# Column-form products in runs: all high parts of the weights first, then all low parts, in a two-layer decoder trunk

## The chip, the cores and the metric

The kernel runs on one core of a Trainium2 chip. The metric is the device time of one execution in microseconds (us). The engines are TensorE (PE, with its weight loads PEld), VectorE (DVE), ScalarE (ACT), GpSimd (POOL) and SyncE (SP), each with an instruction queue of its own that runs in order.

## The reference

256 tokens, model width 1024, one memory of 256 rows, all in float32. Cut to what matters:

```python
# layer 0
h = rms_norm(x, norm_mix[0])
b_gate, c_gate, u = jnp.split(h @ conv_w_in[0], 3, axis=-1)
z = c_gate * u                                  # then a causal conv of width 3 along the tokens
x = x + (b_gate * conv(z)) @ conv_w_out[0]
x = x + mem_cross_attention(rms_norm(x, norm_mem[0]), rms_norm(mem, norm_memkv[0]), ...)   # 4 heads of 256
g, u = jnp.split(rms_norm(x, norm_ffn[0]) @ ffn_w_gu[0], 2, axis=-1)                        # 2 x 2816 columns
x = x + (jax.nn.silu(g) * u) @ ffn_w_down[0]
# one shared K/V from x (8 heads of 128, partial rotary)
# layer 1: block attention over that K/V, then memory attention and SwiGLU as above
return rms_norm(x, norm_final)
```

With 256 tokens there is one block, so the block attention is plain causal attention.

## The kernel before

**Products.** Each float32 weight piece is loaded as `raw` (512 KB, SP's queue) and split in two: `hi`, a rounded copy that ACT writes (a cast), and `lo`, the rest, that DVE writes (raw minus hi). Activations are split in the same way and stand transposed, 128 features on the partitions, in units of four blocks of 128 features (`mix_0`, `mix_1`; in each block the high half and the low half of 256 tokens lie side by side). A product x*w is then x_hi*w_hi + x_lo*w_hi + x_hi*w_lo.

Two forms of product exist. In the row form (`mm3`) tokens come out on the partitions: three products of 256 or 512 columns for each k. In the column form (`mm_cols`, L425) the weights' 128 output columns come out on the partitions. For each of the eight k one product of `hi` with both halves of x (512 columns) and one of `lo` with x's high half (256 columns) are accumulated into one buffer, whose two halves are summed behind it (`col_sum`: an ACT copy of one half, a DVE sum with the other). Column form are the conv's input projection (`cu` for c and u, `pb` for b), the query projection of the memory attention (`q_acc`), and SwiGLU's gate and up (`gu`).

**Buffers.** The `cu` and `gu` accumulations take one of the buffers of the tag `gu`; a buffer is free again when its sum has been made (`side.give("gu")`). `pb` and `q_acc` take another kind, as do the four accumulations of the down projection, `ff_h_b` (token half h, column half b).

**Order of the work.** PE's program is written out in order. What runs beside it (norms, sums, gates, splits of the weights) is written as generators, the "jobs". `side.poll()` behind each product looks at an estimate of every engine's time and issues the next steps of the jobs that are due; the number that a job yields is how many nanoseconds of that estimate it wants to pass before its next step. `act.need(k)` forces out the rest of a job whose result the next product reads. So the order in which ACT and DVE get their instructions follows from this estimate and is fixed when the program is built. Weights are loaded, split high, and split low ahead of their use, as fast as the buffers of raw, hi and lo allow; `feed.free(n)` releases n of them.

**The stages named below.** At the start, the memory `m` is transposed by PE, `hi_memk`/`lo_memk` are made with the norm's gains (`g_cols`, transposed from `g_rows0`), and `acc_memk` (keys of the memory) is computed, while x is loaded and normed (`norm_x`, `in_mix.fill`: `hn` on DVE, transposes `pt_h` on PE, a cast and a subtraction into `mix`). Then come the conv (four pairs `jp` of output column blocks `jj`), the memory attention, and SwiGLU. SwiGLU works on pairs of 128 columns (`gate_up(jp)`); the first two pairs are in the row form, and from the fourth pair on a block of the down projection for an earlier pair (24 products of 512 columns) follows each gate/up pair. Two buffers have the tag `gu`, four are of the other kind.

Of the kernel before, what the change touches and what calls it, by code (L numbers as in the profile page):

```python
# [11 lines left out]
F32 = mybir.dt.float32  # L12
# [7 lines left out]
P = 128  # L20
D = 1024
KD = D // P
T = 256
# [231 lines left out]
def yoco_kernel(  # L255
# [6 lines left out]
    nc = tc.nc  # L262
# [50 lines left out]
    def mm(o, l, r, start, stop, ns):  # L313
        nc.tensor.matmul(o, l, r, start=start, stop=stop)  # L314
        clock.note("pe", ns, [o], [l, r], 200)
# [106 lines left out]
        mm3(acc, act.parts(k, tok(h)), [r[:, 0, bank(b)] for r in w], start, stop)  # L422
        side.poll()

    def mm_cols(acc, act, w, j):  # L425


        for k in range(KD):
            act.need(k)
            x_both = act.units[k // 4][:, k % 4].rearrange("p r t -> p (r t)")  # L430
            hi, lo = (r[:, k % 4, j * P:(j + 1) * P] for r in w[k // 4])
            mm(acc.rearrange("p r t -> p (r t)"), hi, x_both, k == 0, False, 0.4167 * 2 * T + 2)
            side.poll()
            mm(acc[:, 0, :], lo, act.parts(k)[0], False, k == KD - 1, 0.4167 * T + 2)
            side.poll()

    def col_sum(acc, t):
# [116 lines left out]

    load_start(0, (None, nc.scalar))
    g_rows0 = half_tile("g_rows0")[:16, :P]
    load(g_rows0, norm_memkv.rearrange("a (j p) -> (a j) p", p=P), nc.scalar)
    mT0 = new_act("mT0")
    feed.load_to(2)
    load_start(1)  # L560
# [6 lines left out]
        for _ in range(n):  # L567
            transpose(warm[:, :P], ident)

    warm_up(10)  # L570

    def start_transpose(pt, ks):
        for i, k in enumerate(ks):
# [272 lines left out]
    def start_x():  # L846
        in_mix.load_gain()
        for h in range(2):
            for b in range(2):
                load(x_sb[:, h, bank(b)], x[0, tok(h), bank(b)])  # L850

        def norm_x():
            while clock.ready(x_sb[:, 0, bank(0)]) > clock.now:
                yield 200
            for h in range(2):
                for b in range(2):
                    in_mix.fill(h, b)
                    yield 500

        x_job.append(side.start(norm_x()))  # L860

# [9 lines left out]
    def short_conv(act, into):  # L871
        yT = new_act("yT")

        def gate_sum(acc, c):
            yield from col_sum(acc, c)
            side.give("gu")

        def conv(j, acc, pieces, jobs):
            z, u = pieces
            yield from col_sum(acc, u)  # L880
            side.give("gu")
            side.finish(jobs[0])
            vector.tensor_mul(z, z, u)
            side.finish(x_job[1])
            yield
            y = u
            scalar.activation(y, z, AF.Copy, scale=cw[:, 2 * KD + j:2 * KD + j + 1])
            yield
            for i in (1, 2):
                tap = cw[:, (2 - i) * KD + j:(2 - i) * KD + j + 1]  # L890
                vector.scalar_tensor_tensor(y[:, i:], z[:, :T - i], tap, y[:, i:], op0=OP.mult, op1=OP.add)
            yield

        def out_gate(j, acc, pieces, jobs):
# [12 lines left out]
        for jp in range(4):  # L907
            wc, wu, wb = ([feed.take(f"{name}_{jp}_{g}") for g in range(2)] for name in ("wc", "wu", "wb"))
            for jj in range(2):
                j = 2 * jp + jj  # L910
                pieces = [feat.tile([P, T], F32, tag=f"f{i}", name=f"conv{i}") for i in range(2)]
                jobs = []
                for i, w in enumerate((wc, wu)):
                    side.grab("gu")
                    cu = gu_tile("cu")
                    mm_cols(cu, act, w, jj)
                    if jj:
                        feed.free(2)
                    jobs.append(side.start(gate_sum(cu, pieces[i]) if i == 0 else conv(j, cu, pieces, jobs)))
# [34 lines left out]
    def mem_attention(l, kT, values, src, into):  # L954
# [61 lines left out]
        for jp in range(4):  # L1016
            w = [feed.take(f"mq{l}_{jp}_{g}") for g in range(2)]
            side.grab("pair")
            q = pairs.tile([P, 2, 2, T], F32R, tag="pair", name="q")
            q_jobs = []  # L1020
            for dt in range(2):
                acc = acc_tile("q_acc").rearrange("p (r t) -> p r t", r=2)
                mm_cols(acc, act, w, dt)
                if jp == dt == 0:
                    side.start(scales())
                q_jobs.append(side.start(q_part(acc, q, dt)))
            feed.free(2)
            job = side.start(attend(jp, q, q_jobs))
            for h in range(2):
# [4 lines left out]
    def swiglu(l, src, done, fine_end=False, at_end=None):  # L1034
# [45 lines left out]

            guT.add_job(h, jp // 2, side.start(turn()))

        def gate_up(jp):
            w = gu_w(jp)
            for jj in range(2):
                u, j = unit_of(2 * jp + jj)
                pieces = [feat.tile([P, T], F32, tag=f"f{i}", name=f"gu_sb{i}") for i in range(2)]
                gate = None
                for part in range(2):
                    side.grab("gu")  # L1090
                    gu = gu_tile("gu")
                    mm_cols(gu, act, w[part], jj)
                    if jj:
                        feed.free(2)
                    if part == 0:
                        gate = side.start(gate_steps(gu, pieces[0]))
                    else:
                        job = side.start(up_steps(gu, pieces, gate, u[:, j, 0, :], u[:, j, 1, :]))
                for h in range(2):
                    guT.add_job(h, (2 * jp + jj) // 4, job)  # L1100

        def gate_steps(gu, g):
            yield from col_sum(gu, g)
# [33 lines left out]
                    feed.free(4)  # L1137
        accs = [[acc_tile(f"ff{l}_{h}_{b}") for b in range(2)] for h in range(2)]
        steps, last = ffn_steps()
        for kind, jp in steps[ROW_PAIRS:]:  # L1140
            if kind == "gu":
                gate_up(jp)
            else:
                w = down_w(jp)
                for h in range(2):
                    for b in range(2):
                        if h == b == 1:
                            feed.free(2)
# [210 lines left out]
```

## Time and profile before

| | us |
|---|---|
| median of 3 runs | 804.57 |
| lowest and highest | 803.68, 804.71 |
| the profiled execution | 803.24 |
| its span (first to last instruction) | 801.1 |
| PE busy in the span | 792.1 |

The profile is of one execution, 803.24 us long; its rows are times from the start of the span. PE is busy for 99% of the span.

### The profile page before, as it was taken

The numbers are of one execution on the slowest core, as the hardware profiler recorded it, in microseconds if no ns is written. First come the engines' busy times: TensorE is split into PE (matmuls) and PEld (weight loads), VectorE is DVE, ScalarE is ACT, GpSimd is POOL, SyncE is SP. The second block draws the span as 40 slices with busy tenths as digits, with TensorE's granted clock in tenths as the row PEclk, the third lists the DMA queues.
The fourth block names the chain that finished last, engine by engine and source line by source line (L and its number), as shares of the span: only waits on it lengthen the run. The fifth ranks groups of instructions, "written<-read, shape, count | busy, mean of one in ns | idle before, by whom it ended". The sixth has DMA issues, their size and how long they took to land.

```text
span 801.1 us, 11663 instructions
## 1 busy us (share of the span) xinstructions
PE 792.1 (99%) x4493; PEld 689.6 (86%) x4493; DVE 536.9 (67%) x834; ACT 444.2 (55%) x731; POOL 19.4 (2%) x42
## 2 busy tenths in 40 slices
PE   9999999999999999999999999999999999999996
PEld 8988888898998888888888889888989988888885
DVE  5978877775757655666566667777757576556643
ACT  6766555664556545555554566456645565455432
POOL 0200001000000000000000000010000000000000
PEclk9999999999999999999999999999999999999998
DMA  9765656734447665555455316567344476655511
GB/s 330 233 204 183 235 184 211 262 96 138 152 134 247 205 209 163 166 199 197 138 198 203 136 53 228 167 210 260 109 124 154 137 247 209 207 159 173 195 54 52
DMA packets 90219, 143.40 MB, mean 179 GB/s; under 512 B 4844, under 2 KB 70452, under 8 KB 90164
## 3 DMA queue, kind: packets, MB, share of 16 engines
q1 hardware_dynamic: 89700, 141.87, 54.3%
q8 instruction: 35, 0.57, 0.3%
q10 hardware_dynamic: 464, 0.79, 0.3%
q14 instruction: 20, 0.16, 0.1%
HBM read 141.60 MB, written 1.05 MB: 178 GB/s over the span
## 4 chain that ended last, share of the span: by engine, by line
PE 96%; DMA 2%; DVE 1%; ACT 0%; issue 0%; SPq 0%; POOLq 0%; DVEq 0%; ACTq 0%
PE gu L314 31%; PE ff L314 15%; PE cu L314 6%; PE q_acc L314 6%; PE acc_mo L314 6%; PE acc_memv L314 5%; PE acc_memk L314 4%; PE pb L314 3%; PE acc_v L314 3%; PE acc_q L314 3%; PE acc_k L314 3%; PE acc_cout L314 3%; PE acc_o L314 3%; PE po L314 2%; PE s L314 2%; PE pt_h L318 1%
## 5 line engine op out<-in xcount | busy, mean ns | idle before, releaser
L314 PE MATMUL ff<-hi_wd,guT 128*128 128x512 f32 (+1 forms) x352 | 108.1, 387 | 0.0
L314 PE MATMUL gu<-ffn,hi_wu 128*128 128x512 f32 x288 | 103.2, 398 | 0.0
L314 PE MATMUL gu<-ffn,hi_wg 128*128 128x512 f32 x288 | 103.1, 397 | 0.0
L314 PE MATMUL gu<-ffn,lo_wg 128*128 128x256 f32 x288 | 81.0, 281 | 0.0
L314 PE MATMUL gu<-ffn,lo_wu 128*128 128x256 f32 x288 | 80.8, 281 | 0.0
L314 PEld LDWEIGHTS ff<-hi_wd,guT 128*128 128x128 f32 x352 | 65.7, 188 | 13.4
L103 DVE TENSOR_TENSOR gu_sb<-gu_sb,gu 128x256 f32<-128x256 f32 x72 | 30.3, 421 | 69.6 <-ACT gu_sb L103 69.2
L103 ACT CAST hi_wu<-raw_wu 128x1024 fp32r<-128x1024 f32 x52 | 53.4, 1050 | 33.0 <-PE ff L314 25.0
L103 DVE TENSOR_TENSOR lo_wu<-raw_wu,hi_wu 128x1024 fp32r<-128x1024 f32 x52 | 61.7, 1221 | 14.6 <-ACT hi_wu L103 14.6
L314 PE MATMUL ff<-lo_wd,guT 128*128 128x512 f32 (+1 forms) x176 | 68.4, 388 | 0.0
L103 ACT COPY gu_sb<-gu 128x256 f32<-128x256 f32 x72 | 26.8, 373 | 71.4 <-PE gu L314 71.4
L314 PEld LDWEIGHTS gu<-ffn,hi_wu 128*128 128x128 f32 x288 | 54.1, 188 | 13.4
L314 PEld LDWEIGHTS gu<-ffn,hi_wg 128*128 128x128 f32 x288 | 54.1, 188 | 12.9
L103 DVE TENSOR_TENSOR lo_wd<-raw_wd,hi_wd 128x1024 fp32r<-128x1024 f32 x44 | 53.4, 1221 | 10.2 <-ACT hi_wd L103 10.2
L314 PEld LDWEIGHTS gu<-ffn,lo_wg 128*128 128x128 f32 x288 | 54.4, 189 | 0.5
L314 PEld LDWEIGHTS gu<-ffn,lo_wu 128*128 128x128 f32 x288 | 54.4, 189 | 0.0
L103 DVE TENSOR_TENSOR lo_wg<-raw_wg,hi_wg 128x1024 fp32r<-128x1024 f32 x44 | 52.6, 1219 | 1.1 <-ACT hi_wg L103 1.1
L103 ACT CAST hi_wd<-raw_wd 128x1024 fp32r<-128x1024 f32 x44 | 45.8, 1046 | 4.2 <-PE ff L314 4.2
L314 PE MATMUL acc_memk<-mT,hi_memk 128*128 128x256 f32 x256 | 47.2, 289 | 0.0
L103 ACT CAST hi_wg<-raw_wg 128x1024 fp32r<-128x1024 f32 x44 | 45.6, 1051 | 0.6 <-PE acc_mo L314 0.6
L314 PE MATMUL q_acc<-mem,hi_mq 128*128 128x512 f32 x128 | 45.9, 399 | 0.0
L314 PE MATMUL acc_mo<-hi_mo,oT_mem 128*128 128x512 f32 x128 | 41.2, 398 | 0.0
(229 smaller groups left out, 1823.5 us busy)
## 6 DMA issues: line engine op xcount, KB each, us to landing
raw_wg<-in_ffn_w_gu_dram SPq DMA_DIRECT2D x44, 512.0 KB, 4.8
raw_wu<-in_ffn_w_gu_dram SPq DMA_DIRECT2D x44, 512.0 KB, 3.6
raw_wd<-in_ffn_w_down_dram SPq DMA_DIRECT2D x44, 512.0 KB, 4.3
raw_memv<-in_mem_w_kv_dram SPq DMA_DIRECT2D x16, 512.0 KB, 4.5
raw_mq<-in_mem_w_q_dram SPq DMA_DIRECT2D x16, 512.0 KB, 5.1
raw_mo<-in_mem_w_o_dram SPq DMA_DIRECT2D x16, 512.0 KB, 4.9
raw_memk<-in_mem_w_kv_dram SPq DMA_DIRECT2D x14, 512.0 KB, 5.4
raw_wc<-in_conv_w_in_dram SPq DMA_DIRECT2D x8, 512.0 KB, 5.0
```

Source lines behind the costliest of these rows:

```text
L103: return call(out, *args, **kw)
L314: nc.tensor.matmul(o, l, r, start=start, stop=stop)
L318: nc.tensor.transpose(o, i, ident[:i.shape[0], :i.shape[0]])
```

## The change

`mm_cols` gets a `part`: 0 makes all eight products with `hi`, 1 all eight with `lo`. Its callers now fill two or three accumulations side by side: the conv fills both `cu` and `pb` with high products first and then with low ones; the query projection both `q_acc` of a pair; gate and up their two `gu`. `gate_up` is called for one column block at a time, and a down block is cut in two: its half for tokens h = 0 stands where the block stood, and its half for h = 1 between the two column blocks of the next pair. In the start, x's norm yields 2000 instead of 500 between its four steps, there are 13 warm-up transposes instead of 10, `g_rows0` is loaded on SP's queue instead of ACT's, and the first split of `m` stands behind the copy of the gains.

```diff
-    def mm_cols(acc, act, w, j):
+    def mm_cols(acc, act, w, j, part):
         for k in range(KD):
             act.need(k)
-            x_both = act.units[k // 4][:, k % 4].rearrange("p r t -> p (r t)")
-            hi, lo = (r[:, k % 4, j * P:(j + 1) * P] for r in w[k // 4])
-            mm(acc.rearrange("p r t -> p (r t)"), hi, x_both, k == 0, False, 0.4167 * 2 * T + 2)
-            side.poll()
-            mm(acc[:, 0, :], lo, act.parts(k)[0], False, k == KD - 1, 0.4167 * T + 2)
+            wk = w[k // 4][part][:, k % 4, j * P:(j + 1) * P]
+            if part == 0:
+                x_both = act.units[k // 4][:, k % 4].rearrange("p r t -> p (r t)")
+                mm(acc.rearrange("p r t -> p (r t)"), wk, x_both, k == 0, False, 0.4167 * 2 * T + 2)
+            else:
+                mm(acc[:, 0, :], wk, act.parts(k)[0], False, k == KD - 1, 0.4167 * T + 2)
             side.poll()
...
-    load(g_rows0, norm_memkv.rearrange("a (j p) -> (a j) p", p=P), nc.scalar)
+    load(g_rows0, norm_memkv.rearrange("a (j p) -> (a j) p", p=P))
...
-    warm_up(10)
+    warm_up(13)
...
-    start_split(pts[0][:, :2], (0,))
     cols_ps = acc_tile("cols_ps")
     transpose(cols_ps[:, :16], g_rows0)
     side.give("half")
     vector.tensor_copy(g_cols[:, 0, :16], cols_ps[:, :16])
+    start_split(pts[0][:, :2], (0,))
...
                     in_mix.fill(h, b)
-                    yield 500
+                    yield 2000
...
-                jobs = []
+                jobs, cus = [], []
+                for w in (wc, wu):
+                    side.grab("gu")
+                    cus.append(gu_tile("cu"))
+                    mm_cols(cus[-1], act, w, jj, 0)
+                pb = acc_tile("pb").rearrange("p (r t) -> p r t", r=2)
+                mm_cols(pb, act, wb, jj, 0)
                 for i, w in enumerate((wc, wu)):
-                    side.grab("gu")
-                    cu = gu_tile("cu")
-                    mm_cols(cu, act, w, jj)
+                    mm_cols(cus[i], act, w, jj, 1)
...
-                pb = acc_tile("pb").rearrange("p (r t) -> p r t", r=2)
-                mm_cols(pb, act, wb, jj)
+                mm_cols(pb, act, wb, jj, 1)
...
+            gus = []
+            for i in range(2):
+                side.grab("gu")
+                gus.append(gu_tile("gu"))
+                mm_cols(gus[i], act, w[i], jj, 0)
+            for i in range(2):
+                mm_cols(gus[i], act, w[i], jj, 1)
...
         for kind, jp in steps[ROW_PAIRS:]:
             if kind == "gu":
-                gate_up(jp)
+                w = gu_w(jp)
+                gate_up(jp, w, 0)
+                if rest is not None:
+                    down_rest()
+                gate_up(jp, w, 1)
             else:
-                w = down_w(jp)
-                for h in range(2):
-                    for b in range(2):
-                        if h == b == 1:
-                            feed.free(2)
-                        down(jp, w, h, b)
+                rest = jp, down_w(jp)
+                for b in range(2):
+                    down(*rest, 0, b)
+        down_rest()
```

What this does to the order on the engines is seen at three places. The first is PE between a down block and the next gate/up pair in layer 0 (`ff_1_1` is the fourth accumulation of the down block, `hi_wg_4_0` the first half of the k of the gate's weights for pair 4). Before:

```order
L314 MATMUL ff_1_1_2596<-hi_wd_0_2640,guT_0_2378 128x512 x2
L314 MATMUL ff_1_1_2596<-lo_wd_1_2660,guT_0_2378 128x512
L314 MATMUL ff_1_1_2596<-hi_wd_1_2659,guT_0_2378 128x512 x2
L314 MATMUL gu<-ffn_0_2208,hi_wg_4_0_2708 128x512
L314 MATMUL gu<-ffn_0_2208,lo_wg_4_0_2709 128x256
L314 MATMUL gu<-ffn_0_2208,hi_wg_4_0_2708 128x512
```

After:

```order
L314 MATMUL gu<-ffn_0_2211,hi_wg_4_0_2715 128x512 x4
L314 MATMUL gu<-ffn_1_2212,hi_wg_4_1_2735 128x512 x4
L314 MATMUL gu<-ffn_0_2211,hi_wu_4_0_2751 128x512 x4
L314 MATMUL gu<-ffn_1_2212,hi_wu_4_1_2764 128x512 x4
L314 MATMUL gu<-ffn_0_2211,lo_wg_4_0_2716 128x256 x4
L314 MATMUL gu<-ffn_1_2212,lo_wg_4_1_2736 128x256 x4
L314 MATMUL gu<-ffn_0_2211,lo_wu_4_0_2752 128x256 x4
L314 MATMUL gu<-ffn_1_2212,lo_wu_4_1_2765 128x256 x4
L314 MATMUL ff_1_0_2598<-lo_wd_0_2638,guT_0_2390 128x512
L314 MATMUL ff_1_0_2598<-hi_wd_0_2637,guT_0_2390 128x512 x2
L314 MATMUL ff_1_0_2598<-lo_wd_1_2650,guT_0_2390 128x512
L314 MATMUL ff_1_0_2598<-hi_wd_1_2649,guT_0_2390 128x512 x2
```

The alternation of 512 and 256 columns became runs of 16 of each, and `ff_1_0` and `ff_1_1` moved from ahead of the pair to its middle.

The second is DVE around the conv's start (`lo_memk_7` is the last piece of the memory's keys, `mix_0` and `mix_1` the two units of the normed x that every column product of the conv reads, `lo_wc`, `lo_wu`, `lo_wb` the first pair's low parts). Before (behind these rows come the second `lo_wu` and both `lo_wb`):

```order
L103 SCALAR_TENSOR_TENSOR lo_memk_7_423<-raw_memk_7_241,g_cols,hi_memk_7_422 128x1024
L103 COPY m_rsb<-pb_rs 128x256
L103 TENSOR_TENSOR mix_1_291<-pt_h,mix_1_291 128x4x128
L103 TENSOR_TENSOR lo_wc_0_451<-raw_wc_0_272,hi_wc_0_450 128x1024
L103 TENSOR_TENSOR k_sb<-acc_memk_0_179,m_rsb 128x512
L103 TENSOR_TENSOR mix_1_291<-pt_h,mix_1_291 128x4x128
L103 TENSOR_TENSOR memk_u_496<-k_sb,memk_u_496 128x2x256
L103 TENSOR_TENSOR lo_wc_1_473<-raw_wc_1_304,hi_wc_1_472 128x1024
L103 TENSOR_TENSOR lo_wu_0_491<-raw_wu_0_407,hi_wu_0_490 128x1024
```

After (just ahead of these rows stand `lo_memk_7` and two `hn`):

```order
L103 TENSOR_TENSOR mix_1_294<-pt_h,mix_1_294 128x4x128
L103 TENSOR_TENSOR k_sb<-acc_memk_0_182,m_rsb 128x512
L103 TENSOR_TENSOR lo_wc_0_458<-raw_wc_0_275,hi_wc_0_457 128x1024
L103 TENSOR_TENSOR mix_0_293<-pt_h,mix_0_293 128x4x128
L103 TENSOR_TENSOR memk_u_480<-k_sb,memk_u_480 128x2x256
L103 TENSOR_TENSOR k_sb<-acc_memk_1_183,m_rsb 128x512
L103 TENSOR_TENSOR lo_wc_1_475<-raw_wc_1_307,hi_wc_1_474 128x1024
L103 TENSOR_TENSOR lo_wu_0_489<-raw_wu_0_387,hi_wu_0_488 128x1024
L103 TENSOR_TENSOR lo_wu_1_502<-raw_wu_1_413,hi_wu_1_501 128x1024
L103 TENSOR_TENSOR lo_wb_0_587<-raw_wb_0_449,hi_wb_0_586 128x1024
L103 TENSOR_TENSOR lo_wb_1_593<-raw_wb_1_510,hi_wb_1_592 128x1024
L103 TENSOR_TENSOR mix_1_294<-pt_h,mix_1_294 128x4x128
```

The last write of `mix_1` moved from ahead of the second `lo_wc` to behind the second `lo_wb`; two `hn` and a write of `mix_0` now stand behind `lo_memk_7`.

The third is the end of the conv's first pair (`conv_694` and `conv_695` are the sums of the second column block's c and u, `hi_wb_0` and `hi_wb_1` the second pair's weights). On ACT before:

```order
L103 COPY conv_682<-cu 128x256
L103 CAST hi_wb_0_717<-raw_wb_0_592 128x1024
L103 CAST yT_577<-conv_595 128x256
L103 CAST hi_wb_1_737<-raw_wb_1_668 128x1024
L103 COPY conv_683<-cu 128x256
L103 COPY b_sb<-pb 128x256
```

and after:

```order
L103 COPY conv_694<-cu 128x256
L103 CAST hi_wb_0_771<-raw_wb_0_596 128x1024
L103 COPY conv_695<-cu 128x256
L103 COPY b_sb<-pb 128x256
L103 CAST hi_wb_1_789<-raw_wb_1_627 128x1024
```

The cast of `hi_wb_1` moved from ahead of the copy of the second cu to behind the copy of `pb`. On DVE after, at the same place:

```order
L103 TENSOR_TENSOR conv_694<-conv_694,cu 128x256
L103 TENSOR_TENSOR lo_wb_0_772<-raw_wb_0_596,hi_wb_0_771 128x1024
L103 TENSOR_TENSOR lo_wb_1_790<-raw_wb_1_627,hi_wb_1_789 128x1024
L103 TENSOR_TENSOR conv_695<-conv_695,cu 128x256
L103 TENSOR_TENSOR b_sb<-b_sb,pb 128x256
```

Both low parts of `wb` stand between the first sum and the second, whose buffer the next pair's second cu takes.

## Rows read from the trace of the kernel before

**Rows 1.** The page's first part: the span and each engine's busy time, its share and its instructions.
```profile
span 801.1 us, 11663 instructions
PE 792.1 (99%) x4493; PEld 689.6 (86%) x4493; DVE 536.9 (67%) x834; ACT 444.2 (55%) x731; POOL 19.4 (2%) x42
```

**Rows 2.** The page's fourth part: shares of the span by engine in the chain of work that ended last.
```profile
PE 96%; DMA 2%; DVE 1%; ACT 0%; issue 0%; SPq 0%; POOLq 0%; DVEq 0%; ACTq 0%
```

**Rows 3.** Groups of PE's instructions by operands and shape: line, engine, operation, out and in, shape, xcount | busy us, mean ns of one | idle us before.
```profile
L314 PE MATMUL gu<-ffn,hi_wu 128*128 128x512 f32 x288 | 103.2, 398 | 0.0
L314 PE MATMUL gu<-ffn,hi_wg 128*128 128x512 f32 x288 | 103.1, 397 | 0.0
L314 PE MATMUL q_acc<-mem,hi_mq 128*128 128x512 f32 x128 | 45.9, 399 | 0.0
L314 PE MATMUL cu<-mix,hi_wu 128*128 128x512 f32 x64 | 23.0, 399 | 0.0
L314 PE MATMUL cu<-mix,hi_wc 128*128 128x512 f32 x64 | 23.0, 398 | 0.0
L314 PE MATMUL pb<-mix,hi_wb 128*128 128x512 f32 x64 | 22.9, 398 | 0.0
```

**Rows 4.** The timeline of PE: start us, us, engine, line, operation, out and in, shape, xcount. First the alternation in a gate accumulation, then a run of 512-column products in the down block, a run of 256-column products, and two changes of shape.
```profile
300.00 0.40 PE L314 MATMUL gu<-ffn,hi_wg 128*128 128x512 f32 x1
301.06 0.40 PE L314 MATMUL gu<-ffn,hi_wg 128*128 128x512 f32 x1
...
307.27 0.62 PE L314 MATMUL ff<-hi_wd,guT 128*128 128x512 f32 x2
309.31 0.62 PE L314 MATMUL ff<-hi_wd,guT 128*128 128x512 f32 x2
...
31.89 0.40 PE L314 MATMUL acc_memk<-mT,hi_memk 128*128 128x256 f32 x2
32.97 0.40 PE L314 MATMUL acc_memk<-mT,hi_memk 128*128 128x256 f32 x2
...
304.94 0.40 PE L314 MATMUL ff<-lo_wd,guT 128*128 128x512 f32 x1
...
503.54 0.40 PE L314 MATMUL acc_o<-lo_o,oT_moba 128*128 128x512 f32 x1
504.93 0.39 PE L314 MATMUL acc_o<-lo_o,oT_moba 128*128 128x512 f32 x1
```

**Rows 5.** The timeline of DVE and PE around the sixth piece of the memory's keys; in brackets the idle time before an instruction and what ended it.
```profile
19.82 2.73 DVE L103 SCALAR_TENSOR_TENSOR hn<-x_sb,rs,g_mix 128x512 f32<-128x512 f32 x4
...
23.14 0.48 PE L314 MATMUL acc_memk<-mT,hi_memk 128*128 128x256 f32 x2
24.19 0.39 PE L314 MATMUL acc_memk<-mT,lo_memk 128*128 128x256 f32 x1 [0.56 <-DVE lo_memk L103]
```

**Rows 6.** The timeline of DVE, PE and ACT from the last piece of the memory's keys to the conv's first products.
```profile
27.34 1.28 DVE L103 SCALAR_TENSOR_TENSOR lo_memk<-raw_memk,g_cols,hi_memk 128x1024 fp32r<-128x1024 f32 x1
...
29.46 1.22 DVE L103 TENSOR_TENSOR lo_wc<-raw_wc,hi_wc 128x1024 fp32r<-128x1024 f32 x1
30.60 0.69 DVE L103 TENSOR_TENSOR k_sb<-acc_memk,m_rsb 128x512 f32<-128x512 f32 x1
31.21 0.69 DVE L103 TENSOR_TENSOR mix<-pt_h,mix 128x512 fp32r<-128x512 f32 x1
...
34.41 0.40 PE L314 MATMUL cu<-mix,hi_wc 128*128 128x512 f32 x1
...
35.57 1.05 ACT L103 CAST hi_wb<-raw_wb 128x1024 fp32r<-128x1024 f32 x1 [1.08 <-DMA raw_wb<-in_conv_w_in_dram]
```

**Rows 7.** The timeline of PE at the start and at the end, and two stretches of the end: from:to, length, busy us (xcount) of PE, PEld, DVE, ACT and POOL, the granted clock, the DMA share, GB/s.
```profile
1.36 2.40 PE L318 MATMUL warm<-ident 128*128 128x128 f32 x10 [1.36 <-POOL neg_half L519]
...
4.28 0.71 PE L318 MATMUL pt_m<-ident,m 128*128 128x128 f32 x2 [0.53 <-DMA m<-in_mem_dram]
...
6.76 1.78 PE L314 MATMUL acc_memk<-mT,hi_memk 128*128 128x256 f32 x8
...
8.85 1.12 PE L314 MATMUL acc_memk<-mT,hi_memk 128*128 128x256 f32 x8
...
794.16 0.40 PE L314 MATMUL ff_end<-hi_wd,guT 128*128 128x256 f32 x2
...
794.00:796.00 2.00, 0.56 (x5) 0.35 (x3) 0.64 (x2) 0.51 (x2) 0.00 (x0) 1.00 0.00 0
797.00:801.10 4.10, 0.00 (x0) 0.00 (x0) 0.34 (x1) 0.31 (x1) 0.00 (x0) 0.50 0.34 128
```

**Rows 8.** The timeline of PE, ACT and DVE at the end of a gate accumulation.
```profile
302.00 0.28 PE L314 MATMUL gu<-ffn,lo_wg 128*128 128x256 f32 x1
...
302.37 0.37 ACT L103 COPY gu_sb<-gu 128x256 f32<-128x256 f32 x1 [1.10 <-PE gu L314]
...
302.78 0.42 DVE L103 TENSOR_TENSOR gu_sb<-gu_sb,gu 128x256 f32<-128x256 f32 x1 [1.05 <-ACT gu_sb L103]
```

**Rows 9.** The timeline of ACT and of ACT's own queue at the start.
```profile
1.18 0.45 ACTq L331 DMA_DIRECT2D g_rows<-in_norm_memkv_dram  x1
...
11.33 1.15 ACT L103 ACTIVATE hi_memk<-raw_memk,g_cols 128x1024 fp32r<-128x1024 f32 x1 [2.01 <-DMA raw_memk<-in_mem_w_kv_dram]
```

More of the change, by code (lines that the diff above doesn't have):

```diff
@@ L911, in short_conv @@
                 pieces = [feat.tile([P, T], F32, tag=f"f{i}", name=f"conv{i}") for i in range(2)]
-                jobs = []
+                jobs, cus = [], []
[5 more added lines that the diff above has]
+                mm_cols(pb, act, wb, jj, 0)
                 for i, w in enumerate((wc, wu)):
-                    side.grab("gu")
-                    cu = gu_tile("cu")
-                    mm_cols(cu, act, w, jj)
+                    mm_cols(cus[i], act, w, jj, 1)
                     if jj:
                         feed.free(2)
-                    jobs.append(side.start(gate_sum(cu, pieces[i]) if i == 0 else conv(j, cu, pieces, jobs)))
-                pb = acc_tile("pb").rearrange("p (r t) -> p r t", r=2)
-                mm_cols(pb, act, wb, jj)
+                    jobs.append(side.start(gate_sum(cus[0], pieces[0]) if i == 0 else conv(j, cus[1], pieces, jobs)))
+                mm_cols(pb, act, wb, jj, 1)
                 if jj:
@@ L1020, in mem_attention @@
             q_jobs = []
+            accs = []
             for dt in range(2):
-                acc = acc_tile("q_acc").rearrange("p (r t) -> p r t", r=2)
-                mm_cols(acc, act, w, dt)
+                accs.append(acc_tile("q_acc").rearrange("p (r t) -> p r t", r=2))
+                mm_cols(accs[dt], act, w, dt, 0)
                 if jp == dt == 0:
                     side.start(scales())
-                q_jobs.append(side.start(q_part(acc, q, dt)))
+            for dt in range(2):
+                mm_cols(accs[dt], act, w, dt, 1)
+                q_jobs.append(side.start(q_part(accs[dt], q, dt)))
             feed.free(2)
@@ L1081, in gate_up_rows, with gate_up @@
             guT.add_job(h, jp // 2, side.start(turn()))
[L1083 to L1093, printed above, removed]
-                        feed.free(2)
[L1095 to L1098, printed above, removed]
-                for h in range(2):
-                    guT.add_job(h, (2 * jp + jj) // 4, job)
+        def gate_up(jp, w, jj):
+            u, j = unit_of(2 * jp + jj)
+            pieces = [feat.tile([P, T], F32, tag=f"f{i}", name=f"gu_sb{i}") for i in range(2)]
+            gus = []
[5 more added lines that the diff above has]
+                mm_cols(gus[i], act, w[i], jj, 1)
+                if jj:
+                    feed.free(2)
+                if i == 0:
+                    gate = side.start(gate_steps(gus[0], pieces[0]))
+                else:
+                    job = side.start(up_steps(gus[1], pieces, gate, u[:, j, 0, :], u[:, j, 1, :]))
+            for h in range(2):
+                guT.add_job(h, (2 * jp + jj) // 4, job)
         def gate_steps(gu, g):
@@ L1139, in swiglu, with down_rest @@
         steps, last = ffn_steps()
+        rest = None
+        def down_rest():
+            for b in range(2):
+                if b == 1:
+                    feed.free(2)
+                down(*rest, 1, b)
         for kind, jp in steps[ROW_PAIRS:]:
             if kind == "gu":
-                gate_up(jp)
-            else:
-                w = down_w(jp)
-                for h in range(2):
-                    for b in range(2):
-                        if h == b == 1:
-                            feed.free(2)
-                        down(jp, w, h, b)
+                w = gu_w(jp)
[3 more added lines that the diff above has]
+                gate_up(jp, w, 1)
+            else:
+                rest = jp, down_w(jp)
+                for b in range(2):
+                    down(*rest, 0, b)
+        down_rest()
         if at_end is not None:
```

## The prediction

> **What bounds the kernel now.** I read the page's sum of engines first: PE is busy in 792.1 of 801.1 us, DVE in 67% and ACT in 55% [rows 1]. Then the chain that ended last: 96% of it is PE, 2% DMA [rows 2]. So every nanosecond between two products counts, work on ACT and DVE costs nothing while PE's next operand is ready, and every new wait of PE is paid in full. The profiled execution took 803.24 us; the median of three is 804.57, 1.33 us more. I make the sum against 803.24 and add 1.33 at the end.
>
> **The pace of the products (a gain).** The edit touches the column-form products: a high one of 512 columns (both halves of x) and a low one of 256. Before, they alternate. From 300.00 to 301.06 three pairs pass: 353.3 ns a pair. In a run of 512-column products, 307.27 to 309.31 is nine products: 226.7 ns each. In a run of 256-column ones, 31.89 to 32.97 is nine: 120.0 ns each. A pair made of two runs costs 346.7 ns, 6.67 less. There are 288 + 288 + 128 + 64 + 64 + 64 = 896 pairs [rows 3], so runs give 896 x 6.67 = 5.97 us [rows 4].
> Changing shape costs something too: from the alternation into the down block, 304.94 to 307.27, ten products took 2.33 us where ten at 226.7 are 2.27, so 0.06; from a run of 256s into 512s, 503.54 to 504.93, six took 1.39 against 1.36, so 0.03 [rows 4]. About 16 borders of the first kind go and about 52 of the second come: 1.6 - 1.0 = +0.6. Net **-5.4**.
> The Trainium skill (TensorE: Matmul & The Clock Gate, "Back-to-back issue gap") gives a warm gap of N/2.4 + 2.5 ns; a pair would then be 325 ns in either order and the regrouping worth nothing. The rows above disagree with it: both orders are slower than that, and not equal.
>
> **A stall that goes (a gain).** The only one PE has in the first 60 us behind the loads: at 24.19 it had waited for a lo_memk; from the two high products at 23.14 to it are 1.05 us, where two steps at 120 ns and a change of shape would be about 0.35. DVE was in the way with four pieces of hn in a row, 2.73 us from 19.82 [rows 5]. With the wider spacing of x's norm only two stand ahead of that lo_memk. About **-0.7**.
>
> **The start.** Three more warm-up transposes, g_rows on SP's queue and the copy of the gains ahead of the first split all lie ahead of hi_memk at 11.33, which waits for its DMA. That load pins the start, so the gain is zero. Put on SP, g_rows' issue (0.45 us on ACT's queue) delays what SP issues behind it by 0 to 0.45 [rows 9]; I take **+0.2**, since the first big loads are issued ahead of it.
>
> **The conv's start (the largest loss).** The wider steps of the norm move the last write of mix, which the fifth product of cu needs. Before, DVE wrote it at 31.21, ahead of the second lo_wc, and the conv began at 34.41 [rows 6]. In the new order on DVE (shown above) it stands behind both lo_wc, both lo_wu and both lo_wb. From the lo_memk that began at 27.34 I add up the rows: it ends at about 28.3; two hn 1.37 (half of the 2.73 [rows 5]); five of the 0.6 kind (a k_sb to the next start is 30.60 to 31.21: 0.61) 3.0; six low parts at 29.46 to 30.60 = 1.14 each, 6.8; the last mix 0.69. That is 40.2. PE starts the conv 0.7 earlier than before, at 33.7, and after four products is at 34.6. It stands for **5.6** us. Low bound: if DVE's front part is all early, the second k_sb still waits for its acc_memk, which ends 24 products and four transposes (3.3 us) before the conv; then 30.4 + 0.3 + 0.6 + 5 x 1.14 + 0.69 = 37.7, a wait of 3.1. The loads agree: the second hi_wb was cast at 35.57, when its raw_wb had come [rows 6]; + 1.05 + 1.2 + 0.7 = 38.5, a wait of 3.9. High bound 6.5, if lo_memk ends 0.9 later.
> What comes after it is full of finished work, so nothing is won back: before, this work lay under PE.
>
> **The clock behind it.** The first products of acc_memk ran at half pace: eight took 1.78 us at 6.76, and eight 1.12 at 8.85; warm transposes took 2.40 for ten from 1.36. PE had worked unbroken from 4.28, so full pace came some 3.8 us later. At the end PE's last product started at 794.16; the granted clock is 1.00 (2.4 GHz) in 794 to 796 and 0.50 (1.2 GHz) from 797 on, so it fell some 2 us after the end of work [rows 7]. A stand of 5.6 us is longer than that. If the clock falls and 3.8 us run at half pace, 1.9 are lost. I take **+1.7**, bounds 0 and 2.9 (a recovery as long as from the first warm transposes).
>
> **The conv's pair boundaries.** With the three accumulations filled side by side, the next pair's second cu needs the gu buffer which the previous pair's second sum (conv = conv + cu) frees. In the new order DVE has both lo_wb ahead of that sum, and the second lo_wb waits for hi_wb on ACT, which stands behind the copy b_sb, which waits for the end of pb. So from the end of pb: 0.27 + copy 0.37 [rows 8] + hi_wb 1.05 + lo 1.2 [rows 6] + sum 0.42 [rows 8] = 3.3 us. PE covers it with the next pair's eight high products of wc, 8 x 0.2267 = 1.8. It waits about 1.4 at each of three boundaries (jp 0 to 1, 1 to 2, 2 to 3): **+4.2**. Low bound 0, if the weights there come early enough for the casts to be done before pb ends; high 6.
>
> **The FFN.** Between gate/up pairs a gu buffer comes free 1.2 us after the last low product (302.00, copy 302.37, sum 302.78 + 0.42), 1.1 after that product has left PE's queue [rows 8]. In a run of low products the second sum is due when the next gate's high products begin. Where 12 down products lie between (2.7 us), it is hidden; and the half block is enough for that. Where none lies between (three times a layer, the first pairs), the other accumulation's eight low products, 0.96, cover one buffer, and the other is late by 0.15 (1.1 - 0.96) up to 1.2 where a cast is in the way: six times 0.35, near the low end since only some places have a cast there, **+2.1**. At layer 0's first row-form gate/up, two lo_wu casts now stand ahead of ffn's last write on DVE: 2 x 1.14 of which PE's residue covers about half, **+1.2** (0 to 2.9). The q section with its two accumulations at once has a free buffer for each, and its casts stay behind PE: zero, at worst +1.
>
> **Sum.** -5.4 - 0.7 + 0.2 + 5.6 + 1.7 + 4.2 + 2.1 + 1.2 = +8.9: 812.1 profiled, with 1.33 **813.5**. A measurement of this kernel tells about 0.2% (1.6 us) from nothing.
>
> **Rivals.**
> - *Hidden after all (faster).* DVE reaches the last mix in time because the low parts' sources come early and the norm's job is advanced: the conv's wait falls from 5.6 to nothing, with no clock loss, and the boundaries' too. What is left is -5.4 - 0.7 + 0.2 = -5.9, or 798.7. It decides where conv's waits sum to under 6 us. For it: DVE is busy only 67% on average. Against it: the order on DVE is fixed, and from 27.3 to 40 its rows leave no gap [rows 6]. Chance 0.08.
> - *Low bounds everywhere.* 3.1 for the conv's start, no clock loss, 2 for the boundaries, 1 for the rest: -5.9 + 6.1 = +0.2, about 804.7. For it: the clock needs a stretch without work, and the wait may be cut by transposes of pt_c. Chance 0.09.
> - *The clock falls at each boundary of the conv.* 1.7 us more at three places: 818. For it: PE would wait four times within 40 us. Against: waits of 1.4 us, and the fall at the end came about 2 us after the work [rows 7]. Chance 0.12.
> - *The regrouping gives no pace.* If a shape's order made no difference in these products, the 5.4 are missing: 819. The Trainium skill's gap above would make it so. The rows speak against it, since alternation and runs are in one trace [rows 4]. Chance 0.05.
>
> **How the numbers follow.** My forecast has 0.66; its own range is 807.5 to 816.5, from the conv's 3.9 to 6.5, the clock's 0 to 2.9 and the boundaries' 2 to 6. The range 804.0 to 818.5 takes in the low bounds and the clock's case; outside remain the faster rival and the lost pace, 0.13, and tails of the forecast. Faster by over 0.2%: 0.08, and 0.02 of the low-bound case, 0.10. Within 0.2%: half of what the low-bound case has left, 0.04. Slower: 0.86.
>
> **What would show it.** In the trace after: high products of gu 226.7 ns apart and low ones 120 in runs (else the pace is wrong); no wait at the lo_memk near 23; DVE's last mix ending near 40 with PE idle ahead of it for 3 to 6.5 us, and 0.50 as granted clock, or high products 427 ns apart, behind it; three waits of PE for conv's sum at the pair boundaries; six short waits for gu_sb in the FFN. The prediction is wrong if DVE writes the last mix before 35, or if the loads of wb land so much earlier that the casts pass ahead of pb.

## The result and the profile after

The changed kernel takes 814.90 us (median of 4 runs, 814.13 to 816.25) where the kernel before takes 804.63: a ratio of 1.0135, interval [1.0119, 1.0151]. It is 10.3 us slower; 813.5 was forecast. The profiled execution has a span of 812.0 us against 801.1 [rows 1].

The page's span and sum of engines after, and the shares of the chain that ended last:

```profile
span 812.0 us, 11733 instructions
...
PE 792.3 (98%) x4496; PEld 692.1 (85%) x4496; DVE 537.4 (66%) x834; ACT 440.1 (54%) x731; POOL 18.5 (2%) x42
...
PE 92%; DVE 3%; DMA 2%; issue 1%; ACT 1%; POOLq 0%; SPq 0%; ACTq 0%; DVEq 0%
```

DVE, 1% of the chain before [rows 2], now has 3%. PE's waits after say where: engine, line waited for, then the sum in us, how often, the longest.

```profile
PE cu L314 <- DVE mix L103: 5.0, 1, 5.0
PE cu L314 <- DVE conv L103: 3.8, 3, 1.3
...
PE gu L314 <- DVE gu_sb L103: 1.3, 2, 0.7
PE gu L314 <- DVE msp L103: 1.0, 1, 1.0
PE acc_memk L314 <- DVE lo_memk L103: 0.5, 1, 0.5
```

The first two are in the conv. Where it ends is seen in PE's timeline: the first product of its output projection before, and then after.

```profile
102.86 0.40 PE L314 MATMUL acc_cout<-lo_cout,yT 128*128 128x512 f32 x1
```

```profile
113.76 0.40 PE L314 MATMUL acc_cout<-lo_cout,yT 128*128 128x512 f32 x1
```

The conv began at 34.41 before [rows 6] and at 33.76 after (below), so it grew from 68.45 to 80.00 us: 11.55 more, which is more than the 10.9 by which the whole span grew. All the other stages together gave 0.65 back, by the starts of the stages in both traces: 0.65 gained ahead of the conv, 0.55 in the two query projections and 0.3 in the two SwiGLU bodies, 1.0 lost at layer 0's SwiGLU, and small changes at the end.

The conv's start in the timeline of PE and DVE after:

```profile
33.76 1.08 PE L314 MATMUL cu<-mix,hi_wc 128*128 128x512 f32 x4
39.87 0.77 PE L314 MATMUL cu<-mix,hi_wc 128*128 128x512 f32 x1 [5.03 <-DVE mix L103]
42.35 3.62 PE L314 MATMUL cu<-mix,hi_wu 128*128 128x512 f32 x8
45.76 2.34 PE L314 MATMUL pb<-mix,hi_wb 128*128 128x512 f32 x8
...
26.68 1.28 DVE L103 SCALAR_TENSOR_TENSOR lo_memk<-raw_memk,g_cols,hi_memk 128x1024 fp32r<-128x1024 f32 x1
...
34.50 2.35 DVE L103 TENSOR_TENSOR lo_wu<-raw_wu,hi_wu 128x1024 fp32r<-128x1024 f32 x2
36.77 2.36 DVE L103 TENSOR_TENSOR lo_wb<-raw_wb,hi_wb 128x1024 fp32r<-128x1024 f32 x2
39.04 0.69 DVE L103 TENSOR_TENSOR mix<-pt_h,mix 128x512 fp32r<-128x512 f32 x1
```

DVE is never idle from 26.68 to 39.73; its last write of mix ends there, and PE has stood for 5.03 us. Behind it eight products hi_wu take 3.41 us (42.35 to 45.76), 426 ns each where they cost 227 before and later. The clock says why; stretches of the trace after (from:to, length, busy us of PE, PEld, DVE, ACT, POOL, granted clock, DMA share, GB/s):

```profile
33.70:39.80 6.10, 1.14 (x6) 0.63 (x5) 6.10 (x7) 3.93 (x5) 0.00 (x0) 0.99 0.83 243
39.50:39.80 0.30, 0.00 (x0) 0.00 (x0) 0.30 (x2) 0.00 (x0) 0.00 (x0) 0.80 0.77 259
39.87:45.70 5.83, 5.83 (x14) 4.34 (x15) 5.75 (x10) 4.16 (x5) 0.00 (x0) 0.50 1.02 329
45.70:48.00 2.30, 2.30 (x10) 1.84 (x9) 0.80 (x1) 0.00 (x0) 0.00 (x0) 0.82 0.82 248
```

The granted clock fell to 0.50 at about 39.7, in the last 0.2 us of the wait (0.80 over 0.30 us is 0.12 us at half), and was full again at about 46.5 (0.82 over 2.30 us is 0.83 us at half). It was at half for 6.8 us; 6.6 of them lie behind the wait, with PE at work.

A boundary between two of the conv's pairs, in the timeline of PE, ACT and DVE after:

```profile
59.16 2.00 PE L314 MATMUL cu<-mix,hi_wc 128*128 128x512 f32 x8
62.41 2.08 PE L314 MATMUL cu<-mix,hi_wu 128*128 128x512 f32 x8 [1.25 <-DVE conv L103]
...
59.36 0.37 ACT L103 COPY b_sb<-pb 128x256 f32<-128x256 f32 x1 [0.33 <-PE pb L314]
59.63 1.05 ACT L103 CAST hi_wb<-raw_wb 128x1024 fp32r<-128x1024 f32 x1
...
60.71 1.23 DVE L103 TENSOR_TENSOR lo_wb<-raw_wb,hi_wb 128x1024 fp32r<-128x1024 f32 x1 [0.70 <-ACT hi_wb L103]
61.85 0.41 DVE L103 TENSOR_TENSOR conv<-conv,cu 128x256 f32<-128x256 f32 x1
```

It is the chain of the forecast, link by link: end of pb at 59.16, copy, hi_wb, lo_wb, the second sum, and PE at 62.41. From 59.16 to 62.41 are 3.25 us for eight products that cost 1.81: 1.44 lost, and 1.42 at the other two boundaries.

The pace in a steady gate/up block after, and its end:

```profile
303.22 1.98 PE L314 MATMUL gu<-ffn,hi_wg 128*128 128x512 f32 x8
305.03 1.98 PE L314 MATMUL gu<-ffn,hi_wu 128*128 128x512 f32 x8
306.85 1.12 PE L314 MATMUL gu<-ffn,lo_wg 128*128 128x256 f32 x8
307.80 1.12 PE L314 MATMUL gu<-ffn,lo_wu 128*128 128x256 f32 x8
308.76 0.40 PE L314 MATMUL ff<-lo_wd,guT 128*128 128x512 f32 x1
```

16 pairs in 5.54 us are 346 ns a pair, against 353 [rows 4].

### The profile page after: what moved, and what is told of

The parts are those of the page before. It is cut to its first block, busy times and chain, and to the rows that moved or that the text cites. A ratio compares the mean times of both kernels' runs of the same rounds, so it can differ in the third digit from the quotient of the medians.

```text
span 812.0 us, 11733 instructions
## 1 busy us (share of the span) xinstructions
PE 792.3 (98%) x4496; PEld 692.1 (85%) x4496; DVE 537.4 (66%) x834; ACT 440.1 (54%) x731; POOL 18.5 (2%) x42
## 4 chain that ended last, share of the span: by engine, by line
PE 92%; DVE 3%; DMA 2%; issue 1%; ACT 1%; POOLq 0%; SPq 0%; ACTq 0%; DVEq 0%
PE gu L314 28%; PE ff L314 15%; PE q_acc L314 5%; PE acc_mo L314 5%; PE acc_memv L314 5%; PE cu L314 5%; PE acc_memk L314 4%; PE pb L314 3%; PE acc_v L314 3%; PE acc_q L314 3%; PE acc_cout L314 3%; PE acc_o L314 3%; PE acc_k L314 3%; PE po L314 2%; PE s L314 2%; PE pt_h L318 1%
## 5 line engine op out<-in xcount | busy, mean ns | idle before, releaser
L314 PE MATMUL gu<-ffn,hi_wg 128*128 128x512 f32 x288 | 72.5, 393 | 1.4 <-DVE gu_sb L103 1.3
L314 PE MATMUL gu<-ffn,hi_wu 128*128 128x512 f32 x288 | 71.2, 389 | 0.0
L314 PEld LDWEIGHTS gu<-ffn,lo_wg 128*128 128x128 f32 x288 | 39.3, 190 | 2.8
L314 PE MATMUL gu<-ffn,lo_wu 128*128 128x256 f32 x288 | 40.4, 283 | 0.0
L314 PE MATMUL gu<-ffn,lo_wg 128*128 128x256 f32 x288 | 40.2, 282 | 0.0
L314 PE MATMUL acc_memv<-hi_memv,mT 128*128 128x512 f32 x128 | 39.8, 391 | 0.0
L314 PEld LDWEIGHTS acc_memk<-mT,hi_memk 128*128 128x128 f32 x256 | 39.1, 191 | 0.5 <-ACT hi_memk L103 0.4
```

## The experiments

Times are medians; each ratio is to runs of the kernel before on the same chip.

| run | edit | us | ratio to before, 95% |
|---|---|---|---|
| changed kernel | | 814.90 | 1.0135 [1.0119, 1.0151] |
| e1_y500 | norm's spacing undone | 814.51 | 1.0136 [1.0120, 1.0153] |
| e8_conv1 | conv's accumulations one after another | 810.44 | 1.0085 [1.0065, 1.0106] |
| e9_conv1_y500 | both of these | 804.53 | 1.0007 [0.9997, 1.0016] |
| e4_sumnow | second sum ahead of lo_wb | 810.99 | 1.0089 [1.0074, 1.0104] |
| e3_keepwarm | wait for mix filled with transposes | 812.31 | 1.0115 [1.0096, 1.0134] |
| e10_halfwarm | half of it filled | 814.41 | 1.0127 [1.0111, 1.0143] |
| e2_before_y2000 | before, norm's spacing changed | 809.76 | 1.0075 [1.0060, 1.0090] |
| e5_before_runs | before, runs in each accumulation | 801.58 | 0.9970 [0.9957, 0.9982] |
| e6_before_ffn | before, changed SwiGLU | 804.35 | 1.0003 [0.9995, 1.0012] |
| e7_runs_newstart | e5 with the changed start | 801.92 | 0.9977 [0.9968, 0.9986] |

### Is the norm's spacing the cause? (e2_before_y2000 and e1_y500)

```diff
 (kernel before)
                     in_mix.fill(h, b)
-                    yield 500
+                    yield 2000
```

> The kernel before with x's norm yielding 2000; products alternate as before. Theory: the wait comes from the norm's spacing alone. PE reaches the fifth pair of products half a microsecond later than in runs (4 x 0.353 against 4 x 0.227), so it waits some 4.5 us for mix; with the clock falling as in the changed kernel 3 us more are lost, and the wait for lo_memk (0.6) goes: 804.6 + 4.5 + 3 - 0.6 = 811.5; without a fall of the clock 808.5. Rival (the spacing costs only together with the runs): 804 to 805.

It took 809.76 us, 6.5 more than before. The spacing alone, with products alternating as ever, brings the wait; PE's waits in this run, and one stretch (the granted clock is the last number but two):

```profile
PE cu L314 <- DVE mix L103: 4.5, 1, 4.5
```

```profile
40.00:46.00 6.00, 4.87 (x19) 4.02 (x20) 5.22 (x11) 2.81 (x5) 0.00 (x0) 0.72 1.03 330
```

4.5 us as worked out. The clock fell, but half pace lasted only 3.4 us here (0.72 over 6.00 us), so 1.7 were lost and not 3: the time lies between the two given for a fall and for none. The rival (costs only together with runs) has fallen.

The opposite edit, `yield 500` in the changed kernel:

> The changed kernel with x's norm yielding 500 again; all else as changed. Theory (the wider steps put the last write of mix behind six low parts on DVE): the wait of 5.0 us at the conv's fifth product and the half clock behind it (6.4 us at 0.50, some 3.3 lost) go, and the wait for the lo_memk near 23 us (0.6) comes back: 814.9 - 8.3 + 0.6 = about 807. The three waits at the conv's pair boundaries (3.8 in all) stay if they come from the runs alone; part of them goes if DVE's shifted order puts the second sum ahead of the low parts of wb: 803.5 to 807. Rival (the conv waits because its high products in runs reach mix sooner, whatever the norm's spacing): within 1 us of 814.9.

It took 814.51, ratio 1.0136: nothing was won, and the expectation (803.5 to 807) missed by at least 7.5 us. The wait for mix is gone from the trace, as expected; others stand in its place. PE's waits in this run, and then the first one in the timeline, with what ACT did:

```profile
PE cu L314 <- DVE conv L103: 8.0, 5, 3.1
```

```profile
42.26 1.12 PE L314 MATMUL pb<-mix,lo_wb 128*128 128x256 f32 x8
45.24 3.09 PE L314 MATMUL cu<-mix,hi_wc 128*128 128x512 f32 x8 [1.86 <-DVE conv L103]
...
42.56 1.04 ACT L103 CAST hi_wu<-raw_wu 128x1024 fp32r<-128x1024 f32 x1 [0.55 <-DMA raw_wu<-in_conv_w_in_dram]
44.03 0.64 ACT L103 COPY conv<-cu 128x256 f32<-128x256 f32 x2
```

The first `cu` of the block was done at about 41.3, but its copy stands on ACT behind a cast of the next pair's hi_wu, which waited for its load until 42.56; both buffers come free late, and the next block's first product waits until 45.24. Side by side, the sums of a block all fall due at its end, with no product left to cover them, and what stands ahead of them on ACT or DVE is paid by PE. Five such waits make 8.0 us, and the clock fell twice (half pace from 46.1 to 49.5 behind the first, and from 87.0 to 90.4 behind the longest). So the spacing is enough for the wait at mix, but undoing it isn't enough for the conv: PE comes to the block ends earlier, and the loads of the next weights don't (the cast of that hi_wu begins at 42.56 here and at 42.51 in the changed kernel).

### Is the side-by-side order the other cause? (e8_conv1 and e9_conv1_y500)

```diff
-                for w in (wc, wu):
-                    side.grab("gu")
-                    cus.append(gu_tile("cu"))
-                    mm_cols(cus[-1], act, w, jj, 0)
...
+                    cu = gu_tile("cu")
+                    for part in range(2):
+                        mm_cols(cu, act, w, jj, part)
```

> The changed kernel with the conv's accumulations made one after another (each eight high products, then its eight low ones); norm, start, query projection and SwiGLU as changed. Theory: the wait for mix (5.0) and the half clock behind it (3.3) stay, since DVE's order there is the same; the three waits at the pair boundaries (3.8) go, since each sum is due earlier and stands ahead of the low parts of wb: 814.1 - 3.8 = about 810.3. Rival (side by side is the cause of the wait for mix as well): 805 or less.

810.44, as expected: the wait for mix stays at 5.0 and the waits at the boundaries are gone.

> As the run with the conv's accumulations one after another, and x's norm yielding 500. Theory (the norm's spacing and the side-by-side conv each bring waits into the same stage, and either alone keeps most of the loss, as the run with the norm alone undone showed): with both undone the conv stage is that of runs inside each accumulation, 69.3 us, and the whole 814.1 - 3.8 - 5.0 - 3.3 + 0.6 = 802.6. Rival (the loss that the run with the norm undone kept came from elsewhere than the side-by-side sums): 808 or more.

804.53. The conv stage is 68.76 us long (34.77 to 103.53), 11.2 less than in the changed kernel: with both undone its waits are gone but for one of 0.8. The total is 1.9 above what was expected: the stage lost 11.2 and not the 12.1 that I had added up, of which the wait of 0.8 that is left is the most; the conv began 1.0 later (two waits for lo_memk, 1.4 in all) where 0.6 was allowed; and the two SwiGLU bodies took 0.6 longer than in the changed kernel's profile (the longest wait between pairs in layer 0 was 1.06 and not 0.58). These four kernels together settle the place of the loss: 1.0135 with both edits, 1.0136 and 1.0085 with one, 1.0007 with neither.

### The sums at the conv's boundaries (e4_sumnow)

```diff
-            yield from col_sum(acc, u)
+            scalar.copy(u, acc[:, 1, :])
+            vector.tensor_add(u, u, acc[:, 0, :])
+            yield
```

> The changed kernel; in the conv the second accumulation's sum is issued on DVE right behind its copy on ACT, so that it stands ahead of the low parts of wb. Theory (at the three pair boundaries PE waits for that sum, 1.25 us each): the three waits go: 814.9 - 3.8 = about 811.1. Rival (the waits are for the weights themselves, which come no earlier): the waits move to the next product, 814.5 to 815.

810.99: 0.0046 of the ratio, 3.7 us, as expected. No wait for conv is left in the trace, and none took its place in the conv; the weights were there. That the sum stood behind two low parts on DVE, with a cast between, cost the whole.

### The clock's share (e3_keepwarm and e10_halfwarm)

```diff
                     cus.append(gu_tile("cu"))
+                    if w is wc and j == 0:
+                        for _ in range(44):
+                            nc.tensor.transpose(cus[0][:, 0, :P], ident, ident)
```

> The changed kernel with 44 transposes of the identity put into the conv's first accumulation buffer ahead of its first product, which overwrites them. They fill some 4.8 us of the wait for mix with work that nothing needs; the order on DVE and ACT stays. Theory (3.3 of the lost microseconds are the clock's, that fell at the end of the wait): the granted clock stays at 1.00, the first products run at 227 ns, the wait's end stays at 39.9 us: 814.9 - 3.3 = 811.6, up to 1 us less gain if the next pair's sums come late now. Rival (the first products are slow for another reason, operands that arrive late): 814.9, with 450 ns a product as before.

812.31. PE's timeline in this run, and the stretch behind the wait:

```profile
34.10 4.97 PE L919 MATMUL cu<-ident 128*128 128x128 f32 x44
...
40.21 0.47 PE L314 MATMUL cu<-mix,hi_wc 128*128 128x512 f32 x1 [0.21 <-DVE mix L103]
41.64 1.99 PE L314 MATMUL cu<-mix,hi_wu 128*128 128x512 f32 x8
43.47 1.98 PE L314 MATMUL pb<-mix,hi_wb 128*128 128x512 f32 x8
```

```profile
40.00:46.00 6.00, 5.79 (x29) 4.78 (x30) 6.00 (x11) 4.20 (x5) 0.00 (x0) 1.00 1.02 333
```

Mix comes no earlier, but the products behind it run at 229 ns, with the clock at 1.00. From 34.10 to the conv's end at 111.07 are 76.97 us, 3.0 less than the 80.00. The medians say 1.6 (1.0135 to 1.0115, intervals that overlap), the two profiled spans 2.4. So the clock's share is 3.0 by the stage, and the rival (operands late) has fallen.

> The changed kernel with 22 transposes of the identity ahead of the conv's first product, which overwrites them; they fill half of the wait for mix, which is then 2.6 us long. Theory (the clock falls after an idle stretch of 2 us too, as in the run with the norm undone, where half pace lasted 3.4 us): half of the clock's loss goes, 814.1 - 1.6 = about 812.5. Rivals: the clock does not fall, 811; or half pace lasts as long as before, 814.

With 22 transposes the wait for mix was 2.6 us, and half pace lasted as long as behind 5.0; two stretches of this run:

```profile
43.00:46.00 3.00, 3.00 (x8) 2.32 (x8) 3.00 (x5) 2.41 (x3) 0.00 (x0) 0.50 1.00 327
46.00:52.00 6.00, 6.00 (x37) 5.31 (x37) 2.21 (x7) 1.12 (x3) 0.00 (x0) 0.91 0.62 194
```

It began at about 40.2 and ended at about 47.1 (0.91 over 6.00). 814.41: nothing measurable was won, the second rival. What the clock costs did not go with the length of the wait here.

### The pace and the SwiGLU (e5_before_runs and e6_before_ffn)

```diff
 (kernel before, mm_cols)
-        for k in range(KD):
-            act.need(k)
...
+        for part in range(2):
+            for k in range(KD):
+                act.need(k)
+                wk = w[k // 4][part][:, k % 4, j * P:(j + 1) * P]
```

> The kernel before with runs inside each accumulation alone: eight high products, then its eight low ones, and only then the next accumulation; nothing side by side, no half down block, start and norm as before. Theory (a pair in runs costs 346.7 ns against 353.3, and the waits come from filling accumulations side by side): 896 x 6.67 ns = 6.0 less border costs of at most 112 x 0.01 to 0.03 = 1 to 3, and no new wait: 3 to 5.5 us faster than before, ratio 0.993 to 0.996. Rival (the order of shapes makes no difference): ratio 1.000. Second rival (runs inside an accumulation bring the conv's waits too): 1.002 to 1.010.

0.9970 [0.9957, 0.9982]: 2.4 us faster than before by that ratio, less than expected, and the fastest of all these kernels with e7. A gate and up in this run:

```profile
300.05 2.00 PE L314 MATMUL gu<-ffn,hi_wg 128*128 128x512 f32 x8
...
302.84 2.00 PE L314 MATMUL gu<-ffn,hi_wu 128*128 128x512 f32 x8
...
305.64 0.40 PE L314 MATMUL ff<-lo_wd,guT 128*128 128x512 f32 x1
```

16 pairs in 5.59 us: 349 ns a pair, between the alternation's 353 and the 346 of the longer runs. The two SwiGLU stages gained 1.5 and 1.1, the query projections 0.2 and 0.3; the conv became 69.3 (from 68.45) since one wait for conv (0.9) and a shorter one came up there, and layer 1's memory attention got a wait of 0.9 for oT_mem. Shape order does matter, so the rival without a pace gain has fallen; how much of it arrives depends on the sums here too.

The changed SwiGLU alone in the kernel before (gate_up and the half blocks of the diff above, nothing else):

> The kernel before with the changed SwiGLU alone: gate and up side by side in runs, half a down block between. Theory (in the two SwiGLU stages the pace gains 576 x 5.6 ns = 3.2 us and the waits for a gu buffer at the three places of each layer without a down block between cost 1.5 + 1.7 = 3.2): the same as before within 0.5 us, or 1 us slower where the wait at layer 0's first gate/up (1.0) comes along; ratio 0.9995 to 1.0015. Rival (the first sum of the tried forecast, 3.84 of gain against 2.7 of cost): 1.1 us faster, 0.9986.

1.0003 [0.9995, 1.0012]: the same. The pace of 288 pairs a layer is worth up to 2.0 us (288 x 7 ns), and it is spent on the waits between pairs without a down block, 1.4 and 1.6 us in the two layers of the changed kernel (each gap between two products there, less 227 or 120 ns). The largest one of layer 0, in the changed kernel, with PE, DVE and ACT:

```profile
248.24 1.12 PE L314 MATMUL gu<-ffn,lo_wu 128*128 128x256 f32 x8
249.94 1.42 PE L314 MATMUL gu<-ffn,hi_wg 128*128 128x512 f32 x5 [0.58 <-DVE gu_sb L103]
...
249.46 0.75 DVE L103 TENSOR_TENSOR gu_sb<-gu_sb,gu 128x256 f32<-128x256 f32 x2
...
248.11 1.05 ACT L103 CAST hi_wd<-raw_wd 128x1024 fp32r<-128x1024 f32 x1 [0.26 <-DMA raw_wd<-in_ffn_w_down_dram]
249.07 0.70 ACT L103 COPY gu_sb<-gu 128x256 f32<-128x256 f32 x2
```

The gate's low products ended at 248.24, but a cast that had waited for its load held ACT until 249.07, so both copies and both sums came late.

### The start (e7_runs_newstart)

> The runs inside each accumulation as in the run above, with the changed start (13 warm-up transposes, g_rows on SP's queue, the first split behind the copy of the gains); x's norm as before. Theory (the start is pinned by the load that hi_memk waits for): within 0.5 us of the run with runs alone. Rival (three more transposes bring TensorE's full clock earlier): 0.5 to 1 us faster than it.

0.9977 [0.9968, 0.9986], not to be told from e5's 0.9970. The changed start is worth nothing that can be measured.

## Why the prediction was right

The sign, the places and the causes of the terms were as forecast, and the time came within 1.4 us: 814.9 against 813.5. A part of that is luck: between the profiled executions the forecast was 2.0 short (812.1 against 814.1), and the 1.33 that was added for the median is only 0.8 in the changed kernel. The terms by its steps, in us, the measured ones from the profiled execution; the pace is what is left over, so that the sum agrees with the span is no check of it:

| step | forecast | measured | from |
|---|---|---|---|
| pace of the pairs, net | -5.4 | -4.7 | what is left of each stage without its waits: conv 0.8, queries 0.6, SwiGLU 3.3 |
| wait for lo_memk | -0.7 | -0.65 | conv's start, 34.41 to 33.76; 34.10 to 34.26 in e3, e4, e8 and e10, which are the same up to there |
| start | +0.2 | 0 | hi_memk pinned; e7 against e5 |
| wait for mix | +5.6 | +5.0 | PE's idle time (5.2 from start to start); e8, e9 |
| clock behind it | +1.7 | +3.0 | conv's stage with and without it, e3 |
| conv's boundaries | +4.2 | +4.3 | 1.44 + 2 x 1.42; e4 |
| SwiGLU, between pairs | +2.1 | +3.0 | products late in six places, 1.4 and 1.6 a layer |
| SwiGLU, layer 0's start | +1.2 | +1.0 | the wait that ends at 220.19 |
| sum | +8.9 | +11.0 | span: +10.9 |

**The wait for mix** came out 0.6 short since DVE's front part was earlier: its lo_memk ended at 27.96 where 28.3 was taken. The rows in order, each at the time of a like row before, gave the end of mix to half a microsecond (39.73 against 40.2). The place, the writer and the low parts ahead of it are those of the forecast.

**The clock** is the worst-sized term. The fall was forecast, but the 3.8 us of half pace, read from the start of the kernel, were 6.8 here. The upper bound (2.9) just missed the 3.0 that e3 measured; the rows that it was taken from give 3.4, half of the 6.7 us from the first warm transposes at 1.36 to full pace at about 8.1. The rival in which the clock falls at each boundary did not come: the granted clock is 1.00 from 48 on to the end of the stage, through waits of 1.25 us. The boundaries themselves came out as forecast; the forecast's own 3.3 less 1.8 is 1.5 a place, of which it took 1.4, and 1.43 was measured. The bounds that it names for conv, clock and boundaries add up to 807.9 and 817.4, not to its 807.5 and 816.5.

**The SwiGLU's waits** were taken at 0.35 each, near the low end, on the ground that a cast stands in the way at only some places. It does at the first of each layer (0.9 and 1.0), and the other four cost 0.3 each, not 0.15, since behind each such wait the next product came 0.11 late as well. That took the whole pace gain of the stage away, which e6 shows by itself.

**The causes** named are shown for the conv. The clock's loss (e3) and the boundaries (e4) were each taken away alone, and the stage or the time fell by about what the sum gives them. The norm's spacing was put in alone (e2, 6.5 us), and taken away where the conv's accumulations stand one after another (e8 to e9, 0.0078 or 6.3 us, where the wait and the clock make 8.0, less 0.5 for the later start and 0.8 for a wait that came). What the forecast did not see is that undoing the first cause would not have helped: e1 moved 5 us from one wait to five others. The forecast put the wait at mix down to the norm's spacing and the boundary waits to the side-by-side order, and the terms added as if independent; they are so in one direction only. When mix comes early, the same order of sums costs 8.0 instead of 3.8.

**The pace** was 0.7 short: 0.8 of 1.3 arrived in the conv and 3.3 of 3.8 in SwiGLU, the borders not counted; which borders took the rest no run takes apart. The formula of the Trainium skill (TensorE: Matmul & The Clock Gate, "Back-to-back issue gap"), which the page gives for a product taken by itself, would have made the runs worth nothing if it held for this stream of loads and products. In these runs the order of the shapes alone, e5, moved a pair from 353 to 349 ns, and runs of 16 moved it to 346; the measurement decides against it here.

**Layer 0's SwiGLU.** The profile puts PE's wait of 1.0 us there down to msp, a small instruction of the norm, but the product that ends it reads ffn. DVE and PE after:

```profile
218.31 1.22 DVE L103 TENSOR_TENSOR lo_wu<-raw_wu,hi_wu 128x1024 fp32r<-128x1024 f32 x1
219.45 0.69 DVE L103 TENSOR_TENSOR ffn<-pt_h,ffn 128x512 fp32r<-128x512 f32 x1
220.05 0.15 DVE L103 TENSOR_SCALAR msp<-ss 128x1 f32<-128x1 f32 x1
...
220.19 0.50 PE L314 MATMUL gu<-hi_wg,ffn 128*128 128x256 f32 x2 [0.98 <-DVE msp L103]
```

ffn's last write ended at 220.14, behind a lo_wu, and PE went on 0.05 later, before msp had ended: the forecast's mechanism, with one of its two lo_wu right ahead of the write. What moved that lo_wu ahead isn't the SwiGLU's new order alone, where the forecast looked for it: e6, which has that order alone, shows no such wait, nor do e5 and e7, while the changed kernel and the six runs made from it all do (1.0 each). What they share besides is the query projection with its two `q_acc` side by side, which the forecast took at zero; no run has it alone, so whether it needs the SwiGLU's order as well stays open.

## What to carry to other kernels

Grouping products by shape gave a few nanoseconds a pair here, and the buffers' release paid for it: accumulations that are filled side by side finish side by side, so their sums fall due together, in the conv and between SwiGLU pairs without a down block with too few products left to hide them. Write down, for the engine that makes the sums, what stands ahead of them in its order and add it up from the rows; that sum gave the conv's waits to within 0.6 us. Take the runs inside one accumulation (801.58 us here, 0.3% under the kernel before) and leave the buffers' rhythm alone.

## What the runs showed that was not expected

Half pace of TensorE behind a wait lasted either 3.4 us (behind 4.5 us without work in e2, behind 1.9 and 3.1 in e1, behind 1.7 in layer 1's SwiGLU in e8, behind 1.6 at the start of e7) or 6.8 (behind 5.0 in the changed kernel, e4 and e8, behind 2.6 in e10). The length of the wait did not decide it, so a wait halved (e10) won nothing on the clock, while one filled nearly whole (e3) won all of it. Waits of 1.25 us (the boundaries) and one of 1.5 in e1 brought no fall.

Nor did the fall always come as PE went back to work. In the four cases of 6.8 us the granted clock fell before PE went on, by 0.9 us (e4) to 0.01 (e10); in the five of 3.4 it fell after that, by 0.2 (e8) to 1.1 us (e1). The two lengths go with that order in all nine; no run tests why.
